# Low-rank branches from unmixed activations, and scan blocks prepared for two heads at once

## The chip, the cores and the metric

One core of one Trainium2 chip runs the whole program. The metric is the device time of one execution in microseconds. Three runs of the kernel before took 2984.91 to 2988.6 us, median 2986.44.

## The reference, cut to what matters

Two blocks run one after the other on 512 tokens of width 1024, in fp32: a first block of neighbourhood attention, gated convolution and MLP, then two layers, each feed-forward, mixer, feed-forward. The mixer of the first of these layers is RWKV-7 time mixing, and only that is touched here:

```
xx = x_prev - x
xr, xw, xk, xv, xa, xg = [x + xx * mu[i] for i in range(6)]
r, k, v = xr @ w_r, xk @ w_k, xv @ w_v              # 1024 x 1024
w = -softplus(-(w0 + tanh(xw @ w1) @ w2)) - 0.5     # rank 64
a = sigmoid(a0 + (xa @ a1) @ a2)                    # rank 64
g = sigmoid(xg @ g1) @ g2                           # rank 128
...
S = S * w_t + (S @ -kk_t) b_t + v_t k_t             # scan over 512 tokens, 16 heads of 64
y = S @ r_t
```

Each of the six inputs is its own mixture of u = x and d = x_prev - x, with a factor mu per channel.

## The kernel before, in words

Activations lie with channels on partitions: eight chunks of 128 channels, and the time mixing works on two halves of 256 tokens each (`hf`). Large products split both operands into a high and a low fp32r part and use three multiplications; the low-rank products are plain fp32, which the profile shows as two records each.

`rwkv` (L1100) is a set of generators. A planner, `_Emit`, keeps a cost model of each engine, decides when a generator has its next turn, and so fixes the order in which instructions are written; the tile framework then places them. At run time each engine works its queue in that order, and SP issues all DMAs in order. `need` and `until` let other generators run while the main line would wait.

The main line walks through `ORDER` (L1107): for each half K, W, A, R, V, G. `mix_task` (L1160) runs ahead of it and makes the mixtures chunk by chunk. For K, R and V `mix_chunk` makes u + mu d on VectorE in an `h` tile, then ScalarE copies the high part and GpSimd or VectorE subtracts the low one. For W, A and G (the `LORA` branches) it makes the mixture alone, on VectorE, straight into half of a tile of the pool `a`. `lora1` (L1203) multiplies eight such chunks by w1, a1 or g1, eight multiplications a branch. The second factors follow in `decay_task`, `a_task` and `g_task`. `token_major` and `receptance` do K, V and R; their weights come in tiles `wr`, which ScalarE copies to `wh` and VectorE or GpSimd subtracts to `wl`.

Results are spilled to DRAM and fetched again by `prep(q, j)` (L1358): half the heads (`q`) and 128 tokens (`j`), eight in all. Of two heads that share 128 partitions, head `e` lies in partitions 64e to 64e + 63. Per block of 64 tokens (`c`) and per head VectorE makes four products of 64 partitions: r and kk by the decay into `E`, b and k2 by the inverse decay into `bk`, where the two heads' parts stand in opposite order. Tiles `E` are one per head, since their other 64 partitions take the masked products of TensorE afterwards. `inverse(j)` then inverts triangular blocks on GpSimd, by way of DRAM; `scan_task` walks over the blocks; `gn_task` normalizes, and `w_o` projects a half once both scans have come far enough. The pool `a` has 56 tiles; `prep_task` waits until 12 are free.

In the profile nearly all operations other than multiplications carry the line of the helper that records them (L290, L292), so shapes and tile names tell them apart.

Of the kernel before, what the change touches and what calls it, by code (L numbers as in the profile page):

```python
# [20 lines left out]
P = 128  # L21
T = 512
D = 1024
DC = D // P
# [10 lines left out]
_VEC = {}  # L35
# [262 lines left out]
def tile_net(ctx: ExitStack, tc: tile.TileContext, a: dict, out: bass.AP, dbg=None, stop=None):  # L298
# [34 lines left out]
    def S():  # L333
        return spool.tile([P, 64], F32, tag="s", name=nm("s"))
# [762 lines left out]
    def rwkv(on_h):  # L1097
# [2 lines left out]
        live[0] = BEFORE  # L1100

        ud = {}
        oka, half_tile = S(), [None]
        vt.tensor_scalar(out=oka[:, 0:8], in0=vec[:, _VEC["k_a"] : _VEC["k_a"] + 8], scalar1=-1.0, scalar2=1.0, op0=MUL, op1=ADD)
        R_, W_, K_, V_, A_, G_ = range(6)
        LORA = {W_: ("w1", 64), A_: ("a1", 64), G_: ("g1", 128)}

        ORDER = [(0, K_), (0, W_), (0, A_), (0, R_), (0, V_), (0, G_), (1, K_), (1, W_), (1, A_), (1, R_), (1, V_), (1, G_)]
        LAST_A = [x for x in ORDER if x[0] == 0][-1]
        mixed = {x: [] for x in ORDER}  # L1110
        made, used, flags = [0], [0], {}
        AHEAD = 8
        EARLY = 10
        MARGIN = [2]
        turn = [0]

# [4 lines left out]
        def mix_chunk(i, c, hf):  # L1121

            uc, dc, m = ud[hf, c][:, 0:256], ud[hf, c][:, 256:512], V("mu", 8 * i + c)
            if i in LORA:
                if c % 2 == 0:
                    half_tile[0] = A()
                t_ = half_tile[0][:, HALF[c % 2]]
                vt.scalar_tensor_tensor(out=t_, in0=dc, scalar=m, in1=uc, op0=MUL, op1=ADD)
                return (t_,)
            t_ = H()  # L1130
            vt.scalar_tensor_tensor(out=t_, in0=dc, scalar=m, in1=uc, op0=MUL, op1=ADD)
            x_ = A(F32R)
            hi, lo = x_[:, 0:256], x_[:, 256:512]
            split_into((hi, lo), t_, HW, eng=vt if c % 3 == 2 else gp)
            return hi, lo
# [22 lines left out]
                free(*h, n=2)  # L1158

        def mix_task():  # L1160
            for hf, i in ORDER:
                for c in range(DC):
                    while made[0] >= used[0] + (AHEAD if (hf, i) in ORDER[:4] else 8) or (hf, c) not in ud or not room(MARGIN[0]):
                        yield 0.25
                    mixed[hf, i].append(mix_chunk(i, c, hf))
                    made[0] += i not in LORA or c % 2
                    if hf == 1 and i == ORDER[-1][1]:
                        free(ud[1, c])
                    if hf == 0 and (hf, i) == LAST_A:
                        free(ud[0, c])  # L1170
                    yield mixed[hf, i][max(c - 2, 0)]

        for hf in range(2):
# [26 lines left out]
            mixed[hf, i] = None  # L1200
            return pss

        def lora1(w, m, hf, i):  # L1203
            ps = PS()
            for k in range(DC):
                x_ = take(hf, i, k)[0]
                w_ = w[k * m // 512][:, k * m % 512 : k * m % 512 + m]
                em.need(ps[:m, HW], w_, x_)
                mm(ps[:m, HW], w_, x_, k == 0, k == DC - 1)
                if k % 2:  # L1210
                    used[0] += 1
                    free(x_)
            mixed[hf, i] = None
            return ps

        def kkrow(wh):
# [58 lines left out]
            free(x_)  # L1275
            flags["lg", hf] = True

        def load_raw(src, n, rows=P):

            ts = [A() for _ in range(0, n, 512)]  # L1280
            for i, t_ in enumerate(ts):
                dma(out=t_[:rows, :], in_=src[:, 512 * i : 512 * i + 512])
            return ts

        def lora2(hf, w, rows, mid, done_):
            ws = load_raw(a[w], 1024, rows)
            for n in range(DC):
                p2 = PS()
                w_ = ws[n // 4][0:rows, (n % 4) * 128 : (n % 4 + 1) * 128]
                yield (p2, w_, mid)  # L1290
                mm(p2[:, HW], w_, mid[0:rows, :])
                done_(n, p2)
            free(*ws)

        def a_task(hf, ps):

            x_ = A()
            mid = x_[:, HW]
            copy(mid[0:64, :], ps[0:64, HW])

            def fin(n, p2):
                t_ = H()
                act.activation(out=t_, in_=p2[:, HW], func=AF.Sigmoid, bias=V("a0", n))
                spill(ad[hf][n], t_)

            yield from lora2(hf, "a2", 64, mid, fin)
            free(x_)
            flags["a", hf] = True

        def g_task(hf, ps):  # L1310

            x_ = A()
            mid = x_[:, HW]
            act.activation(out=mid, in_=ps[:, HW], func=AF.Sigmoid)

            def fin(n, p2):
                t_ = H()
                copy(t_, p2[:, HW])
                spill(gd[hf][n], t_)

            yield from lora2(hf, "g2", 128, mid, fin)
            free(x_)
            flags["g", hf] = True

# [33 lines left out]
        def prep(q, j):  # L1358
# [25 lines left out]
            F[q, j], ARB[q, j] = ff, rb_t  # L1384
            f4 = ff.rearrange("p (c q f) -> p c q f", c=2, q=4)
            rb4 = rb_t.rearrange("p (c q f) -> p c q f", c=2, q=4)
            for c in range(2):
                bk, cg = A(), 2 * j + c
                b4 = bk.rearrange("p (q f) -> p q f", q=4)
                for e in range(2):  # L1390
                    pr = slice(64 * e, 64 * e + 64)
                    ee = A()
                    E[q, e, cg] = ee
                    e4 = ee.rearrange("p (q f) -> p q f", q=4)
                    tt(vt, e4[pr, :, 64:128], tv(r_, pr, c), tv(pp_, pr, c), MUL)
                    tt(vt, e4[pr, :, 1:64], tv(kk, pr, c, 1, 64), tv(pp_, pr, c, 0, 63), MUL)
                    copy(e4[pr, :, 0:1], tv(kk, pr, c, 0, 1))
                    ob, ok = (0, 64) if e == 0 else (64, 0)
                    tt(vt, b4[pr, :, ob : ob + 64], tv(b_, pr, c), tv(ip, pr, c), MUL)
                    tt(vt, b4[pr, :, ok : ok + 64], tv(k2, pr, c), tv(ip, pr, c), MUL)  # L1400
                    yield [k2,]
                yield (bk, *(E[q, e, cg] for e in range(2)))
                pas = [PS(), PS()]
                for p in range(4):
                    for e in range(2):
                        pr = slice(64 * e, 64 * e + 64)
# [12 lines left out]
                copy(BKN[q, cg], pn)  # L1419
                free(bk)  # L1420
            free(kk, b_, ip, pp_)
            f8 = ff.rearrange("p (u f) -> p u f", u=8)
            for e in range(2):
                for b in range(2):
# [93 lines left out]
        def prep_task():  # L1518
            for n in range(8):
                j, q = n // 2, n % 2  # L1520
                hf = j // 2
                while not all(flags.get(n_) for n_ in (("k", hf, q), ("lg", hf), ("a", hf), ("r", hf, q))):
                    yield 0.3
                while n >= prepped[0] + 2 or not room(12):
                    yield 0.3
                em.spawn(prep(q, j))
                yield 0.3
# [191 lines left out]
            free(*(zq[hf, k][i] for k in range(4) for i in range(2)))  # L1719
            em.spawn(post(hf, o, hs, so))  # L1720

        tasks = {W_: decay_task, A_: a_task, G_: g_task}
        raw = {}
        for n, (hf, i) in enumerate(ORDER):
            for nxt in ORDER[n : n + 2]:
                if nxt[1] in LORA and nxt not in raw:
                    w, m = LORA[nxt[1]]
                    raw[nxt] = load_raw(a[w], 8 * m)
            if not hv and n >= EARLY and min(done["z"]) >= 1:
                w_o(0)  # L1730
            if i in LORA:
                em.spawn(tasks[i](hf, lora1(raw[hf, i], LORA[i][1], hf, i)))
                free(*raw[hf, i])
            elif i == K_:
                em.spawn(keys_task(hf, token_major(a["w_k"], K_, hf)))
            elif i == V_:
# [329 lines left out]
def pack(inp):  # L2066
# [46 lines left out]
    w["w_k"] = _wn(rkv[1])  # L2113
    w["w_v"] = _wn(rkv[2])
    w["rwkv_w_o"] = _wt(g["rwkv_w_o_2"][0])
    w["w1"] = _wn(g["rwkv_w1_2"][0], 64)[0]
    w["w2"] = np.ascontiguousarray(np.concatenate([g["rwkv_w2_2"][0], g["rwkv_w0_2"][0][None]], axis=0))
    w["a1"] = _wn(g["rwkv_a1_2"][0], 64)[0]
    w["a2"] = np.ascontiguousarray(g["rwkv_a2_2"][0])
    w["g1"] = _wn(g["rwkv_g1_2"][0], 128)[0]  # L2120
    w["g2"] = np.ascontiguousarray(g["rwkv_g2_2"][0])
# [28 lines left out]
```

## Time and profile before

| | |
|---|---|
| median of three runs | 2986.44 us |
| profiled execution | 2986.91 us |
| its span | 2985.1 us |
| TensorE busy (x: instructions) | 2820.6 us, 94% (x17736) |
| VectorE busy | 1624.0 us, 54% (x2896) |
| ScalarE busy | 1233.9 us, 41% (x2141) |
| GpSimd busy | 692.3 us, 23% (x802) |
| mean granted TensorE clock | 0.968 |

The shares are means over the whole program; the time mixing takes a part of it with shares of its own. In the profile PE is TensorE, DVE is VectorE, ACT is ScalarE, POOL is GpSimd, SP issues the DMAs. A granted clock of 1.0 is 2.4 GHz, 0.5 is 1.2 GHz.

### The profile page before, as it was taken

To read this page: it belongs to the slowest core of one execution; us is meant where nothing else is said; L and a number is where in the kernel's file an instruction comes from. 1 tells how busy PE (TensorE), PEld (TensorE's weight loads), DVE (VectorE), ACT (ScalarE), POOL (GpSimd) and SP (SyncE) were. 2 spreads that over 40 slices of the span, in tenths; PEclk is the share of its full clock that TensorE was granted. 3 is DMA by queue.
4 is the path that set the end of the run, shared out by engine and by line. 5 is a ranking of instruction groups with operands and counts; after the bars stand their busy time and mean duration, and the time that the engine had idled before them with its cause. 6 is when DMAs were issued, how large, how long until landed. Compare 5 with 4: busy or idle time off the path is not lost. (4 is left out here: it accounts for less than half of the span.)

```text
span 2985.1 us, 45687 instructions
## 1 busy us (share of the span) xinstructions
PE 2820.6 (94%) x17736; PEld 2442.6 (82%) x17736; DVE 1624.0 (54%) x2896; ACT 1233.9 (41%) x2141; POOL 692.3 (23%) x802
## 2 busy tenths in 40 slices
PE   9999999999999989878789989998999989999998
PEld 7788888889888877656679989998888877888887
DVE  6545443335334486955676665366234476852336
ACT  4532333333333345544455544344233347733333
POOL 0022211111111143444355110111111134420111
PEclk9999999999999999988889999999999999999999
DMA  5333333332333455645565556343334432323334
GB/s 187 88 94 97 114 99 99 98 95 81 108 99 121 121 184 185 205 142 159 166 177 167 179 168 180 111 145 111 98 98 122 124 114 75 102 80 101 111 109 155
DMA packets 179408, 378.31 MB, mean 127 GB/s; under 512 B 57204, under 2 KB 81908, under 8 KB 179192
## 3 DMA queue, kind: packets, MB, share of 16 engines
q1 hardware_dynamic: 179192, 375.40, 41.6%
q8 instruction: 140, 2.29, 0.3%
q14 instruction: 76, 0.62, 0.1%
HBM read 342.04 MB, written 29.36 MB: 124 GB/s over the span
## 5 line engine op out<-in xcount | busy, mean ns | idle before, releaser
L379 PE MATMUL m<-a,wh 128*128 128x256 f32 (+1 forms) x8512 | 2061.5, 334 | 15.1 <-DVE a L290 7.2
L379 PEld LDWEIGHTS m<-a,wh 128*128 128x128 f32 x8512 | 1461.6, 192 | 178.7 <-issue 13.9
L379 PE MATMUL m<-a,wl 128*128 128x256 f32 (+1 forms) x4256 | 1414.1, 333 | 2.9 <-DVE wl L290 2.9
L290 ACT ACTIVATE wh<-wr 128x1024 fp32r<-128x1024 f32 (+2 forms) x585 | 606.0, 1038 | 1190.7 <-PE m L379 714.8
L290 DVE TENSOR_TENSOR wl<-wr,wh 128x1024 fp32r<-128x1024 f32 (+2 forms) x547 | 679.7, 1244 | 458.9 <-ACT wh L290 456.0
L379 PEld LDWEIGHTS m<-a,wl 128*128 128x128 f32 x4256 | 815.8, 192 | 78.4 <-DVE wl L290 3.5
L290 POOL TENSOR_TENSOR a<-a,a 128x256 f32<-128x256 f32 (+5 forms) x312 | 359.6, 1159 | 1633.5 <-ACT a L290 1317.4
L290 DVE TENSOR_TENSOR a<-m,a 128x512 f32<-128x512 f32 (+1 forms) x324 | 198.5, 614 | 629.6 <-PE m L379 618.9
L290 ACT ACTIVATE a<-a 128x512 f32<-128x512 f32 (+6 forms) x515 | 239.6, 481 | 121.3 <-DVE a L290 88.9
L379 PE MATMUL m<-wh,a 128*128 128x512 f32 x800 | 268.0, 409 | 12.5 <-DVE a L290 10.3
L379 PEld LDWEIGHTS m<-wh,a 128*128 128x128 f32 x800 | 155.7, 195 | 49.3 <-DVE a L290 12.5
L290 DVE TENSOR_TENSOR a<-a,a 128x256 f32<-128x256 f32 (+3 forms) x305 | 164.2, 567 | 36.0 <-ACT a L290 28.9
L379 PE MATMUL m<-wl,a 128*128 128x512 f32 x400 | 162.5, 406 | 0.0
L290 DVE SCALAR_TENSOR_TENSOR a<-a,vec,a 128x256 fp32r<-128x256 f32 (+4 forms) x246 | 144.9, 629 | 9.2 <-ACT a L290 8.4
L290 POOL TENSOR_TENSOR a<-h,a 128x256 fp32r<-128x256 f32 x80 | 68.3, 856 | 342.6 <-ACT a L290 328.0
L290 POOL TENSOR_TENSOR wl<-wr,wh 128x1024 fp32r<-128x1024 f32 x38 | 95.0, 2502 | 110.3 <-ACT wh L290 103.2
L379 PE MATMUL t<-a,a 64*128 64x128 f32 (+4 forms) x528 | 90.0, 356 | 32.0 <-DVE a L290 16.5
L379 PEld LDWEIGHTS t<-a,a 64*128 64x128 f32 (+3 forms) x528 | 57.4, 198 | 56.5 <-issue 25.6
L290 ACT ACTIVATE a<-t 128x512 f32<-128x512 f32 (+3 forms) x122 | 59.3, 491 | 90.0 <-PE t L379 70.6
L379 PEld LDWEIGHTS m<-wl,a 128*128 128x128 f32 x400 | 78.1, 195 | 16.1 <-issue 0.7
L290 ACT ACTIVATE a<-a,vec 128x256 fp32r<-128x256 f32 (+2 forms) x108 | 60.3, 565 | 47.2 <-DVE a L290 43.1
L292 ACT ACTIVATE a<-t 128x256 f32<-128x256 f32 (+3 forms) x100 | 45.4, 472 | 80.3 <-PE t L379 60.6
(108 smaller groups left out, 1533.5 us busy)
## 6 DMA issues: line engine op xcount, KB each, us to landing
wr<-in_ffn_w_in_dram SPq DMA_DIRECT2D x204, 512.0 KB, 3.7
wr<-in_ffn_w_out_dram SPq DMA_DIRECT2D x80, 448.0 KB, 3.3
wr<-in_ffn_w_out_dram SPq DMA_DIRECT2D x48, 512.0 KB, 3.6
wr<-in_w_out_t_dram SPq DMA_DIRECT2D x34, 512.0 KB, 3.7
wr<-in_w_mlp_in_dram SPq DMA_DIRECT2D x32, 512.0 KB, 3.6
wr<-in_w_mlp_out_dram SPq DMA_DIRECT2D x32, 512.0 KB, 3.7
wr<-in_w_gate_dram SPq DMA_DIRECT2D x16, 512.0 KB, 3.6
wr<-in_w_k_dram SPq DMA_DIRECT2D x16, 512.0 KB, 4.6
```

The source lines that it names most:

```text
L290: return fn(*args, **kw)
L292: return fn(*args, **kw)
L379: nc.tensor.matmul(out_, lhsT=lhsT, rhs=rhs, start=start, stop=stop)
```

## The change

w1 and a1 become one matrix of 128 columns, and the three low-rank branches no longer get mixtures. With x = u + mu d, x @ w1 = u @ w1 + d @ (mu w1): GpSimd multiplies the raw weights by mu once a half (`lora_w`), and TensorE multiplies u and d each by its matrix into one PSUM tile. W and A share the step `WA_`; the a branch then lies in partitions 64 to 127, and `a_task` and `lora2` work there. The u and d tiles of a half are freed after G's products instead of its mixtures.

In `prep` b and k2 are multiplied by the inverse decay once for all blocks and heads; the products for `E` are made for both heads in one instruction, into the first head's tile; ScalarE copies the upper half to the second head's tile and places the four parts of `bk`. `prep_task` waits for 13 free tiles.

```diff
-        ORDER = [(0, K_), (0, W_), (0, A_), (0, R_), (0, V_), (0, G_), (1, K_), (1, W_), (1, A_), (1, R_), (1, V_), (1, G_)]
+        WA_ = 6
+        ORDER = [(hf, i) for hf in range(2) for i in (K_, WA_, R_, V_, G_)]
+        MIXED = [x for x in ORDER if x[1] in (K_, R_, V_)]
...
-        EARLY = 10
+        EARLY = 8
...
-            if i in LORA:
-                if c % 2 == 0:
-                    half_tile[0] = A()
-                t_ = half_tile[0][:, HALF[c % 2]]
-                vt.scalar_tensor_tensor(out=t_, in0=dc, scalar=m, in1=uc, op0=MUL, op1=ADD)
-                return (t_,)
...
+        def lora_w(name, idx):
+            ws = load_raw(a[name], 1024)
+            ms = []
+            for i, w_ in enumerate(ws):
+                m_ = A()
+                w4, m4 = (t_.rearrange("p (k i m) -> p k i m", k=4, i=len(idx)) for t_ in (w_, m_))
+                for x, id_ in enumerate(idx):
+                    c = _VEC["mu"] + 8 * id_ + 4 * i
+                    mu = vec[:, c : c + 4].unsqueeze(2).broadcast_to([P, 4, 128 // len(idx)])
+                    tt(gp, m4[:, :, x, :], w4[:, :, x, :], mu, MUL)
+                ms.append(m_)
+            return ws, ms
+
+        def lora1(hf, ws, ms):
             ps = PS()
             for k in range(DC):
-                x_ = take(hf, i, k)[0]
-                w_ = w[k * m // 512][:, k * m % 512 : k * m % 512 + m]
-                em.need(ps[:m, HW], w_, x_)
-                mm(ps[:m, HW], w_, x_, k == 0, k == DC - 1)
...
+                em.until(lambda: (hf, k) in ud)
+                for i, t_ in enumerate((ws, ms)):
+                    w_, x_ = t_[k // 4][:, (k % 4) * 128 : (k % 4 + 1) * 128], ud[hf, k][:, HALF[i]]
+                    em.need(ps[:, HW], w_, x_)
+                    mm(ps[:, HW], w_, x_, k == 0 and i == 0, k == DC - 1 and i == 1)
+            free(*ws, *ms)
             return ps
...
+            ki = A()
+            tt(vt, b_, b_, ip, MUL)
+            tt(vt, ki, k2, ip, MUL)
+            free(ip)
+            yield [ki,]
+            both = slice(0, 128)
             for c in range(2):
-                bk, cg = A(), 2 * j + c
+                bk, e0, e1, cg = A(), A(), A(), 2 * j + c
+                tt(vt, e4[:, :, 64:128], tv(r_, both, c), tv(pp_, both, c), MUL)
+                tt(vt, e4[:, :, 1:64], tv(kk, both, c, 1, 64), tv(pp_, both, c, 0, 63), MUL)
+                copy(e4[:, :, 0:1], tv(kk, both, c, 0, 1))
                 for e in range(2):
                     pr = slice(64 * e, 64 * e + 64)
-                    tt(vt, e4[pr, :, 64:128], tv(r_, pr, c), tv(pp_, pr, c), MUL)
-                    tt(vt, e4[pr, :, 1:64], tv(kk, pr, c, 1, 64), tv(pp_, pr, c, 0, 63), MUL)
-                    copy(e4[pr, :, 0:1], tv(kk, pr, c, 0, 1))
                     ob, ok = (0, 64) if e == 0 else (64, 0)
-                    tt(vt, b4[pr, :, ob : ob + 64], tv(b_, pr, c), tv(ip, pr, c), MUL)
-                    tt(vt, b4[pr, :, ok : ok + 64], tv(k2, pr, c), tv(ip, pr, c), MUL)
-                    yield [k2,]
+                    copy(b4[pr, :, ob : ob + 64], tv(b_, pr, c))
+                    copy(b4[pr, :, ok : ok + 64], tv(ki, pr, c))
+                copy(e1[64:128, :], e0[64:128, :])
...
-                while n >= prepped[0] + 2 or not room(12):
+                while n >= prepped[0] + 2 or not room(13):
...
         for n, (hf, i) in enumerate(ORDER):
+            if i == K_:
+                lw[WA_] = lora_w("wa1", (W_, A_))
+            elif i == V_:
+                lw[G_] = lora_w("g1", (G_,))
...
+            if i == WA_:
+                ps = lora1(hf, *lw[WA_])
+                em.spawn(decay_task(hf, ps))
+                em.spawn(a_task(hf, ps))
+            elif i == G_:
+                em.spawn(g_task(hf, lora1(hf, *lw[G_])))
+                free(*(ud[hf, c] for c in range(DC)))
```

## Rows read from the trace of the kernel before

**Rows 1.** Windows: stretch, length, busy us (x) by engine, PEclk, DMA share, GB/s
```profile
1060.00:1180.00 120.00, 98.93 (x548) 81.08 (x547) 92.83 (x173) 56.81 (x104) 50.64 (x48) 0.90 0.55 178
1180.00:1290.00 110.00, 84.92 (x445) 67.49 (x443) 93.60 (x166) 52.40 (x112) 56.30 (x84) 0.91 0.59 184
1290.00:1480.00 190.00, 154.80 (x1561) 120.49 (x1562) 115.15 (x244) 91.68 (x191) 78.76 (x121) 0.81 0.56 165
1480.00:1600.00 120.00, 106.12 (x1109) 95.10 (x1108) 92.97 (x201) 68.69 (x150) 71.42 (x120) 0.89 0.61 176
1060.00:1600.00 540.00, 444.77 (x3657) 364.16 (x3656) 394.55 (x784) 269.59 (x555) 257.12 (x371) 0.87 0.58 174
```

**Rows 2.** Waits of PE, 1060 to 1600: total us, times, longest us
```profile
PE t L379 <- DVE a L290: 23.2, 13, 4.8
PE t L379 <- ACT a L290: 14.6, 2, 13.7
PE m L379 <- DVE a L290: 14.1, 6, 7.0
PE m L379 <- ACT a L290: 11.9, 3, 9.6
PE t L379 <- POOL a L290: 5.5, 1, 5.5
PE t L393 <- DVE a L290: 4.2, 2, 2.1
PE t L393 <- POOL a L292: 4.2, 2, 2.4
PE t L379 <- DVE h L290: 4.0, 3, 1.9
```

**Rows 3.** Groups by shape, DVE, 1060 to 1740: busy us, mean ns, idle before
```profile
L290 DVE TENSOR_TENSOR a<-a,a 64x256 f32<-64x256 f32 x96 | 43.6, 478 | 0.7 <-DMA bon<-a 0.2
L290 DVE SCALAR_TENSOR_TENSOR a<-a,vec 128x256 f32<-128x256 f32 x48 | 27.1, 595 | 0.1
L290 DVE TENSOR_TENSOR a<-a,a 64x252 f32<-64x252 f32 x32 | 21.4, 670 | 0.0
L290 DVE TENSOR_TENSOR a<-a,a 128x512 f32<-128x512 f32 x8 | 7.6, 954 | 15.7 <-ACT a L290 15.7
```

**Rows 4.** Groups by shape, ACT, 1060 to 1740
```profile
L290 ACT ACTIVATE a<-a 128x256 f32<-128x256 f32 x46 | 18.4, 409 | 9.0 <-DVE a L290 8.7
L290 ACT ACTIVATE a<-a 128x512 f32<-128x512 f32 x24 | 14.7, 624 | 9.4 <-DMA a<-lg 6.5 <-DVE a L290 2.9
L290 ACT ACTIVATE a<-a 64x4 f32<-64x4 f32 x32 | 6.5, 202 | 2.2 <-DMA bon<-a 1.8
```

**Rows 5.** Groups by shape, POOL, 1060 to 1740
```profile
L290 POOL TENSOR_TENSOR a<-a,a 128x256 f32<-128x256 f32 x28 | 26.2, 938 | 28.0 <-ACT a L290 27.2
L292 POOL TENSOR_TENSOR a<-a,s 128x512 f32<-128x512 f32 x16 | 20.0, 1250 | 38.5 <-DVE s L292 30.9 <-ACT a L292 6.0 <-ACT wh L290 1.5
```

**Rows 6.** Timeline of PE, low-rank products, half 0: start us, us, idle before
```profile
1131.45 7.12 PE L379 MATMUL m<-a,a 128*64 128x256 f32 x32 [2.18 <-DVE a L290]
...
1235.61 5.46 PE L379 MATMUL m<-a,a 128*128 128x256 f32 x16 [2.00 <-ACT a L290]
```

**Rows 7.** Timeline of DVE and POOL around 1200 us
```profile
1197.65 5.00 DVE L290 TENSOR_TENSOR a<-a,a 64x256 f32<-64x256 f32 x8
...
1199.09 2.60 POOL L290 TENSOR_TENSOR wl<-wr,wh 128x1024 fp32r<-128x1024 f32 x1 [4.51 <-DMA wr<-in_w_v_dram]
...
1221.48 2.87 DVE L290 TENSOR_TENSOR a<-a,a 64x256 f32<-64x256 f32 x8
```

**Rows 8.** Timeline of ACT and PE around 1290 us
```profile
1291.79 1.06 ACT L290 ACTIVATE wh<-wr 128x1024 fp32r<-128x1024 f32 x1 [12.06 <-DMA wr<-in_w_r_dram]
...
1293.61 2.66 PE L379 MATMUL t<-a,a 64*128 64x128 f32 x14 [13.71 <-ACT a L290]
```

**Rows 9.** DMA issues: out<-in, KB each, median us to landing
```profile
a<-in_w_dram SPq DMA_DIRECT2D x2, 256.0 KB, 5.2
```

More of the change, by code (lines that the diff above doesn't have):

```diff
@@ L1102, in rwkv @@
         ud = {}
-        oka, half_tile = S(), [None]
+        oka = S()
         vt.tensor_scalar(out=oka[:, 0:8], in0=vec[:, _VEC["k_a"] : _VEC["k_a"] + 8], scalar1=-1.0, scalar2=1.0, op0=MUL, op1=ADD)
         R_, W_, K_, V_, A_, G_ = range(6)
-        LORA = {W_: ("w1", 64), A_: ("a1", 64), G_: ("g1", 128)}
-        ORDER = [(0, K_), (0, W_), (0, A_), (0, R_), (0, V_), (0, G_), (1, K_), (1, W_), (1, A_), (1, R_), (1, V_), (1, G_)]
-        LAST_A = [x for x in ORDER if x[0] == 0][-1]
-        mixed = {x: [] for x in ORDER}
+        WA_ = 6
+        ORDER = [(hf, i) for hf in range(2) for i in (K_, WA_, R_, V_, G_)]
+        MIXED = [x for x in ORDER if x[1] in (K_, R_, V_)]
+        mixed = {x: [] for x in MIXED}
         made, used, flags = [0], [0], {}
         AHEAD = 8
-        EARLY = 10
+        EARLY = 8
         MARGIN = [2]
@@ L1160, in mix_task @@
         def mix_task():
-            for hf, i in ORDER:
+            for hf, i in MIXED:
                 for c in range(DC):
-                    while made[0] >= used[0] + (AHEAD if (hf, i) in ORDER[:4] else 8) or (hf, c) not in ud or not room(MARGIN[0]):
+                    while made[0] >= used[0] + (AHEAD if (hf, i) in MIXED[:2] else 8) or (hf, c) not in ud or not room(MARGIN[0]):
                         yield 0.25
                     mixed[hf, i].append(mix_chunk(i, c, hf))
[L1166 to L1170, printed above, removed]
+                    made[0] += 1
                     yield mixed[hf, i][max(c - 2, 0)]
@@ L1201, in token_major @@
             return pss
-        def lora1(w, m, hf, i):
+        def lora_w(name, idx):
[11 more added lines that the diff above has]
+        def lora1(hf, ws, ms):
             ps = PS()
             for k in range(DC):
-                x_ = take(hf, i, k)[0]
-                w_ = w[k * m // 512][:, k * m % 512 : k * m % 512 + m]
-                em.need(ps[:m, HW], w_, x_)
-                mm(ps[:m, HW], w_, x_, k == 0, k == DC - 1)
[L1210 to L1213, printed above, removed]
+                em.until(lambda: (hf, k) in ud)
[4 more added lines that the diff above has]
+            free(*ws, *ms)
             return ps
@@ L1276, in decay_task, with load_raw @@
             flags["lg", hf] = True
-        def load_raw(src, n, rows=P):
+        def load_raw(src, n, rows=slice(0, P)):
             ts = [A() for _ in range(0, n, 512)]
             for i, t_ in enumerate(ts):
-                dma(out=t_[:rows, :], in_=src[:, 512 * i : 512 * i + 512])
+                dma(out=t_[rows, :], in_=src[:, 512 * i : 512 * i + 512])
             return ts
@@ L1288, in lora2 @@
                 p2 = PS()
-                w_ = ws[n // 4][0:rows, (n % 4) * 128 : (n % 4 + 1) * 128]
+                w_ = ws[n // 4][rows, (n % 4) * 128 : (n % 4 + 1) * 128]
                 yield (p2, w_, mid)
-                mm(p2[:, HW], w_, mid[0:rows, :])
+                mm(p2[:, HW], w_, mid[rows, :])
                 done_(n, p2)
@@ L1298, in a_task @@
             mid = x_[:, HW]
-            copy(mid[0:64, :], ps[0:64, HW])
+            copy(mid[64:128, :], ps[64:128, HW])
             def fin(n, p2):
@@ L1304, in fin @@
                 spill(ad[hf][n], t_)
-            yield from lora2(hf, "a2", 64, mid, fin)
+            yield from lora2(hf, "a2", slice(64, 128), mid, fin)
             free(x_)
@@ L1319, in fin @@
                 spill(gd[hf][n], t_)
-            yield from lora2(hf, "g2", 128, mid, fin)
+            yield from lora2(hf, "g2", slice(0, 128), mid, fin)
             free(x_)
@@ L1386, in prep @@
             rb4 = rb_t.rearrange("p (c q f) -> p c q f", c=2, q=4)
-            for c in range(2):
-                bk, cg = A(), 2 * j + c
-                b4 = bk.rearrange("p (q f) -> p q f", q=4)
+            ki = A()
[4 more added lines that the diff above has]
+            both = slice(0, 128)
+            for c in range(2):
+                bk, e0, e1, cg = A(), A(), A(), 2 * j + c
+                E[q, 0, cg], E[q, 1, cg] = e0, e1
+                b4, e4 = (t_.rearrange("p (q f) -> p q f", q=4) for t_ in (bk, e0))
+                tt(vt, e4[:, :, 64:128], tv(r_, both, c), tv(pp_, both, c), MUL)
+                tt(vt, e4[:, :, 1:64], tv(kk, both, c, 1, 64), tv(pp_, both, c, 0, 63), MUL)
+                copy(e4[:, :, 0:1], tv(kk, both, c, 0, 1))
                 for e in range(2):
                     pr = slice(64 * e, 64 * e + 64)
-                    ee = A()
-                    E[q, e, cg] = ee
-                    e4 = ee.rearrange("p (q f) -> p q f", q=4)
-                    tt(vt, e4[pr, :, 64:128], tv(r_, pr, c), tv(pp_, pr, c), MUL)
-                    tt(vt, e4[pr, :, 1:64], tv(kk, pr, c, 1, 64), tv(pp_, pr, c, 0, 63), MUL)
-                    copy(e4[pr, :, 0:1], tv(kk, pr, c, 0, 1))
                     ob, ok = (0, 64) if e == 0 else (64, 0)
-                    tt(vt, b4[pr, :, ob : ob + 64], tv(b_, pr, c), tv(ip, pr, c), MUL)
-                    tt(vt, b4[pr, :, ok : ok + 64], tv(k2, pr, c), tv(ip, pr, c), MUL)
-                    yield [k2,]
+                    copy(b4[pr, :, ob : ob + 64], tv(b_, pr, c))
+                    copy(b4[pr, :, ok : ok + 64], tv(ki, pr, c))
+                copy(e1[64:128, :], e0[64:128, :])
                 yield (bk, *(E[q, e, cg] for e in range(2)))
@@ L1420, in prep @@
                 free(bk)
-            free(kk, b_, ip, pp_)
+            free(kk, b_, ki, pp_)
             f8 = ff.rearrange("p (u f) -> p u f", u=8)
@@ L1720, in w_o @@
             em.spawn(post(hf, o, hs, so))
-        tasks = {W_: decay_task, A_: a_task, G_: g_task}
-        raw = {}
+        lw = {}
         for n, (hf, i) in enumerate(ORDER):
[L1725 to L1728, printed above, removed]
+            if i == K_:
+                lw[WA_] = lora_w("wa1", (W_, A_))
+            elif i == V_:
+                lw[G_] = lora_w("g1", (G_,))
             if not hv and n >= EARLY and min(done["z"]) >= 1:
                 w_o(0)
-            if i in LORA:
-                em.spawn(tasks[i](hf, lora1(raw[hf, i], LORA[i][1], hf, i)))
-                free(*raw[hf, i])
+            if i == WA_:
[5 more added lines that the diff above has]
+                free(*(ud[hf, c] for c in range(DC)))
             elif i == K_:
@@ L2115, in pack @@
     w["rwkv_w_o"] = _wt(g["rwkv_w_o_2"][0])
-    w["w1"] = _wn(g["rwkv_w1_2"][0], 64)[0]
+    w["wa1"] = _wn(np.concatenate([g["rwkv_w1_2"][0], g["rwkv_a1_2"][0]], axis=1), 128)[0]
     w["w2"] = np.ascontiguousarray(np.concatenate([g["rwkv_w2_2"][0], g["rwkv_w0_2"][0][None]], axis=0))
-    w["a1"] = _wn(g["rwkv_a1_2"][0], 64)[0]
     w["a2"] = np.ascontiguousarray(g["rwkv_a2_2"][0])
```

## The prediction

> **What bounds the kernel now.** I read the busy time by stretches first, then who ended TensorE's waits in the same stretch, then the rows of the operations that the change touches, by shape. Over the whole span TensorE is the bound. The part that the change touches, 1060 to 1600 us (the time mixing's projections and the first scans), is another matter: TensorE is busy 444.77 of 540 us there, so 95.2 us are idle, at a granted clock of 0.87 [rows 1]. The reader is to see in the four stages that VectorE is busy 92.83 of 120, 93.60 of 110, 115.15 of 190 and 92.97 of 120 us, ScalarE about half of each. In the second stage VectorE is the fullest engine of all.
>
> Who ended TensorE's idle time [rows 2]: VectorE 23.2 + 14.1 + 4.2 + 4.0 = 45.5 us, which is 48% of the 95.2. ScalarE ended 14.6 + 11.9 = 26.5 us, but in one case each of 13.7 and 9.6 us it was only the last of a chain. Ahead of the 13.7 us ScalarE itself had waited 12.06 us for a weight tile of w_r [rows 8]: the load stood in SP's queue, so its cause is a transfer issued late. That leaves some 3 of 26.5 for plain ScalarE work, and with the 9.6 us about 13%; I work with 11%. GpSimd ended 5.5 + 4.2 = 9.7 us (10%); as it often stands behind ScalarE and VectorE in a chain I take 20%.
>
> The lost clock is a second price of the same waits. Busy time times what is missing of full clock, by stage: 98.93 x 0.10 + 84.92 x 0.09 + 154.80 x 0.19 + 106.12 x 0.11 = 58.6 us [rows 1], or 0.62 us for each idle microsecond. If half of that goes with the idle time that goes, an idle microsecond saved is worth 1.31.
>
> **The change part by part.**
>
> *Mixtures of the low ranks (removed).* 48 VectorE instructions, mean 595 ns: 27.1 us [rows 3]. Half 0's and half 1's share of w and a is 16 each, of g 8 each.
>
> *Block preparation on VectorE.* Eight preparations, all before 1600 us, now issue 96 products of 64x256 at 478 ns and 32 of 64x252 at 670 ns: 43.6 + 21.4 = 65.0 us [rows 3]. After: per preparation two whole products (b and k2 by the inverse decay), 16 x 954 ns = 15.3 us by the row of 128x512, and per block one product for both heads in place of two. Twice the partitions are no more elements per partition, so I price them by the 64-partition rows: 16 x 478 ns = 7.6 us and 16 x 670 ns = 10.7 us. Sum 33.6, so 31.4 us less. VectorE loses 27.1 + 31.4 = 58.5 us of its 394.55. What this is worth to TensorE lies between nothing (each VectorE-ended wait is taken over by the next late thing) and all 45.5 us. I take the 48% share: 58.5 x 0.48 = 28.1 us. Late next where these waits go are the weight splits, whose loads SP issues late [rows 8], and GpSimd's block inverses.
>
> *Placing on ScalarE (added).* Per block four copies of 64x256 and one of 64x512, and one small copy instead of two: 64 x 409 ns = 26.2, 16 x 624 ns = 10.0, minus 16 x 202 ns = 3.2, together 33.0 us [rows 4]. It is also a new wait: the products go from VectorE through ScalarE before TensorE may begin. Behind the copies in ScalarE's queue stand the high parts of the weight splits (VectorE's low parts and then TensorE wait for them) and the PSUM evacuations. The ends are 0 (ScalarE is busy only 269.59 of 540 us [rows 1]) and all 33.0; with the 11% share I charge 3.6 us.
>
> *Scaled weights on GpSimd (added).* Per half four multiplications of 128x256 elements for w and a, two of 128x512 for g: 8 x 938 ns + 4 x 1250 ns = 12.5 us [rows 5]. Ends 0 and 12.5, charged at 20%: 2.5 us. GpSimd also waits for the raw weights to land. The same bytes are loaded in the same number of DMAs as before, but a1's now comes with w1's; a load takes 5.2 us to land [rows 9], and behind the waiting multiplication on GpSimd stand its share of K's weight splits and mixture splits, for which TensorE waits. Four loads make 0 to 21 us of standing, at 20% up to 4.2 us; I take 0, since each pair of matrices is asked for a whole projection ahead.
>
> The row that speaks most against this part is VectorE beside GpSimd. Eight products of 64x256 took 5.00 us while GpSimd ran a split of 2.60 us at 1199.09, and 2.87 us at 1221.48 [rows 7], 0.62 against 0.36 us each. The Trainium skill ("GPSIMD Engine Reference", section "Specifications") says that GpSimd shares its SBUF interfaces with VectorE, and that VectorE instructions with two SBUF inputs contend with it. The trace agrees, and by that rule the 12.5 us would also be taken from VectorE; that is a rival below.
>
> *TensorE.* w and a together keep their 16 multiplications per half, now of 128 columns instead of 64 (32 records in 7.12 us [rows 6]); g goes from 8 to 16 per half, 32 records more in all. At 7.12/32 us a record that is 7.1 us, at g's own 5.46/16 (part of it at the low clock) 10.9. I take 9.0. No mixture has to be ready for them any more; what that saves is in VectorE's share already.
>
> *The rest at nothing.* The a branch in the upper 64 partitions changes no count; the order of projections stays as it was with w and a in one step, and the output projection may start at the same step. The u and difference tiles of a half are held until g's multiplications instead of its last mixture: at most g's 5.46 us [rows 6] later, which a preparation that waits for 13 free tiles would see. It is covered as long as the scan has a finished block ahead. Uncovered it is 5.5 us, once a half.
>
> **Sum.** Idle time: -28.1 + 3.6 + 2.5 = -22.0 us. Clock: 0.31 x 22.0 = -6.8. TensorE's work: +9.0. Together -19.8 us. The profiled execution took 2986.91 us (2985.1 span and 1.8 around it), 0.5 over the median of the three runs, 2986.44. So 2967.1 on the one and 2966.6 on the other; I say 2967. With VectorE's share between 0.35 and 0.7 this case reaches from 2977 (-20.5 + 6.1 idle, x 1.31, + 9) to 2950 (-41.0 + 6.1).
>
> **Rivals.**
>
> A, the waits go altogether: all 45.5 us, and the 13.7 us stall too, because an earlier inverse no longer holds SP's queue. (-59.2 + 6.1) x 1.31 + 7.1 = -62.5, 2924 us. For it: VectorE is fullest just ahead of that stall. Against: the planner lays the order anew, and such a stall can as well appear elsewhere.
>
> B, hidden: only a fifth of the VectorE time reaches TensorE, since ScalarE's, GpSimd's and SP's waits lie just behind. (-11.7 + 6.1) x 1.31 + 9 = +1.7, 2989 us. For it: the third stage is the one with the most idle time (35.2 us), and VectorE is busy only 61% of it [rows 1]; only stages one and two are clearly its own.
>
> C, slower: ScalarE takes over as the engine that is late in the preparation. With a share x of the 33.0 us reaching TensorE the sum is 1.31 x (-28.1 + 2.5 + 33.0x) + 9 = -24.5 + 43.2x. It decides from x = 0.57: beyond that the kernel is slower, at 0.8 it takes 2997, at 1 it takes 3006. For it: every block's two parts now pass ScalarE's one queue, next to weight splits of about 1 us each [rows 8]. Against: ScalarE is busy 52.40 of 110 us in the second stage, 48%, and 33.0 us over the whole 540 add 6%.
>
> D, GpSimd's multiplications block VectorE for their whole length: VectorE saves 46 instead of 58.5 us, 12.5 x 0.48 x 1.31 = 7.9 us less gain, 2975 us. The contended row bears it out in part: the products there lost 2.1 us beside a split of 2.6 us [rows 7]. It is what the rule of the Trainium skill named above would come to at its worst.
>
> **How the numbers follow.** Forecast 0.42, A (below 2950) 0.14, B (2981 to 2993) 0.17, C (above 2993) 0.17, D 0.10. A measurement of this kernel can tell about 0.2% from no change, 6 us. Faster by more than that holds the forecast, A and D: 0.66; within it B: 0.17; slower C: 0.17. The range leaves out the far ends of A and C, about 0.1 each: 2935 to 2998. The forecast's own is 2950 to 2977.
>
> **What would show it.** The mixture rows of 128x256 into a full tile gone (48), the 64x256 and 64x252 products gone, VectorE's busy time about 58 us lower and ScalarE's 33, GpSimd's 12 higher. In the stretch of the projections, TensorE's waits ended by VectorE down from 45.5 to about 20 us, the clock there up. After it the profile should be as before, shifted. Wrong would be: VectorE lower by that much and TensorE's idle time unchanged (B), waits now ended by ScalarE in the preparation's multiplications (C), or a longer stall behind SP's queue.

## The result, and the profile after

The changed kernel takes 3006.89 us (median, 3001.99 to 3010.78), the kernel before 2987.09 in the same comparison: ratio 1.0066, 95% interval 1.0048 to 1.0084. Forecast was 2967, range 2935 to 2998. It is slower, by nearly what it was to gain.

The profiled execution's span went from 2985.1 to 3002.7 us, by 17.6: TensorE's busy time grew by 7.8 (2820.6 to 2828.4), its idle time by 9.8. VectorE is busy 43.1 us less over the whole span, ScalarE 28.0 and GpSimd 4.4 more.

Busy time by stretches, after; columns as in [rows 1]:
```profile
1060.00:1180.00 120.00, 92.45 (x509) 76.75 (x508) 89.01 (x157) 54.05 (x100) 52.75 (x51) 0.84 0.52 172
1180.00:1290.00 110.00, 96.99 (x513) 80.75 (x512) 75.12 (x109) 73.25 (x150) 74.63 (x94) 0.92 0.67 211
1290.00:1480.00 190.00, 150.61 (x1403) 121.82 (x1401) 97.32 (x191) 104.86 (x229) 69.82 (x114) 0.83 0.56 169
1480.00:1600.00 120.00, 88.89 (x1122) 79.47 (x1121) 79.93 (x183) 55.89 (x130) 70.33 (x134) 0.82 0.46 124
```
Only the second stage, where VectorE had been the fullest engine, has more of TensorE at work (84.92 to 96.99 us). The first lost 6.5 us, the third 4.2, the fourth 17.2.

Who ended TensorE's waits there, after, for [rows 2]:
```profile
PE m L379 <- POOL a L290: 13.5, 4, 9.9
PE t L379 <- DVE a L290: 12.2, 5, 5.7
PE t L379 <- ACT a L290: 11.4, 8, 7.6
PE t L379 <- DVE s L292: 10.5, 2, 9.0
PE m L379 <- ACT a L290: 10.1, 5, 3.0
PE t L379 <- DVE h L292: 9.2, 2, 6.1
PE t L393 <- POOL a L292: 8.5, 1, 8.5
PE t L379 <- DMA a<-in_g_dram: 7.3, 2, 5.6
PE m L379 <- DVE a L290: 6.1, 3, 3.0
```
VectorE's two largest rows fell from 37.3 to 18.3 us, but not its sum. [rows 2] shows only the first eight rows of the view; over all rows VectorE ended 50.6 us before and 43.4 after, ScalarE 33.9 and 30.2, GpSimd 9.9 and 27.9, DMAs 0.4 and 9.1. Single long waits have come, ended by a different engine each time, which points to something late upstream of all of them.

The operations themselves, after, by shape, VectorE first; for [rows 3], [rows 4] and [rows 5]. The mixtures that stayed stand in the first row; before, they had
```profile
L290 DVE SCALAR_TENSOR_TENSOR h<-a,vec 128x256 f32<-128x256 f32 x48 | 27.8, 608 | 1.7 <-POOL a L290 1.2
```
and after:
```profile
L290 DVE SCALAR_TENSOR_TENSOR h<-a,vec 128x256 f32<-128x256 f32 x48 | 39.2, 850 | 17.9 <-POOL a L290 13.6 <-ACT a L290 3.9
L290 DVE TENSOR_TENSOR a<-a,a 128x256 f32<-128x256 f32 x55 | 31.9, 589 | 1.9 <-ACT a L290 1.9
L290 DVE TENSOR_TENSOR a<-a,a 128x512 f32<-128x512 f32 x24 | 19.0, 806 | 16.1 <-ACT a L290 16.0
L290 DVE TENSOR_TENSOR a<-a,a 128x252 f32<-128x252 f32 x16 | 8.4, 528 | 0.0
...
L290 ACT ACTIVATE a<-a 64x256 f32<-64x256 f32 x64 | 23.0, 404 | 0.4
L290 ACT ACTIVATE a<-a 64x512 f32<-64x512 f32 x16 | 9.9, 618 | 13.7 <-DVE a L290 13.6
...
L290 POOL TENSOR_TENSOR a<-a,vec 128x512 f32<-128x512 f32 x4 | 6.2, 1565 | 0.7 <-DMA a<-in_g_dram 0.7
L290 POOL TENSOR_TENSOR a<-a,vec 128x256 f32<-128x256 f32 x8 | 5.4, 707 | 2.1 <-DMA a<-in_wa_dram 2.1
```
The counts are those of the forecast and the prices near it: ScalarE's placing 32.9 us (forecast 36.2 before the small copies), GpSimd's scaling 11.6 (12.5).

The view that shows the cause is SP's queue, at the issues that begin a preparation (`a<-kkt`, the key fetch) and a block inverse (`iat<-fsc`). Before, the fourth fetch and the second inverse (start us, us to issue):
```profile
1264.44 0.38 SPq L290 DMA_DIRECT2D a<-kkt  x1
...
1306.24 2.94 SPq L290 DMA_DIRECT2D iat<-fsc  x2
```
After, the third and fourth fetch, then the second inverse:
```profile
1252.16 0.38 SPq L290 DMA_DIRECT2D a<-kkt  x1
...
1329.49 0.63 SPq L290 DMA_DIRECT2D a<-kkt  x1
...
1363.20 1.10 SPq L290 DMA_DIRECT2D iat<-fsc  x2
```
The third fetch is 38 us late (before it was at 1213.96), the fourth 65, the inverse 57. The projections meanwhile run ahead: g's last low-rank product begins at 1417.36 instead of 1474.71. TensorE then waits, first in a projection, later in preparations, the scan and what follows it (timeline of TensorE, idle before in brackets):
```profile
1388.80 1.22 PE L379 MATMUL m<-wh,a 128*128 128x512 f32 x2 [9.90 <-POOL a L290]
...
1447.09 3.33 PE L379 MATMUL t<-a,a 64*128 64x128 f32 x16 [7.61 <-ACT a L290]
...
1506.16 1.11 PE L393 MATMUL t<-cst,a 128*128 128x128 f32 x4 [8.52 <-POOL a L292]
...
1573.08 0.99 PE L379 MATMUL t<-cst,a 128*128 128x1 f32 x4 [9.00 <-DVE s L292]
```
The first of these waits shows one way in which the lateness is paid. The product is one of V's, and it waits for a mixture split (`a<-h,a`) on GpSimd. ScalarE had done its part of that mixture at 1378.11, but the split stood in GpSimd's queue behind operations of the second block inverse (`h<-a,iat`), which now falls into this projection (timeline of GpSimd):
```profile
1387.67 0.40 POOL L290 TENSOR_TENSOR h<-a,iat 128x120 f32<-128x120 f32 x1
1388.03 0.72 POOL L290 TENSOR_TENSOR a<-h,a 128x256 fp32r<-128x256 f32 x1
```
Before, all of TensorE's waits of this kind (`PE m <- POOL a`) came to 0.2 us from 1060 to 1600.

### The profile page after: what moved, and what is told of

Same layout as the page of the kernel before. It is cut to its first block, busy times and chain, and to the rows that moved or that the text cites. A ratio compares the mean times of both kernels' runs of the same rounds, so it can differ in the third digit from the quotient of the medians.

```text
span 3002.7 us, 45719 instructions
## 1 busy us (share of the span) xinstructions
PE 2828.4 (94%) x17768; PEld 2458.4 (82%) x17768; DVE 1580.9 (53%) x2768; ACT 1261.9 (42%) x2205; POOL 696.7 (23%) x814
## 4 chain that ended last, share of the span: by engine, by line
PE 77%; DVE 9%; POOL 4%; issue 4%; ACT 3%; DMA 2%; SPq 1%; DVEq 0%; ACTq 0%; POOLq 0%
PE m L379 70%; PE t L379 5%; DVE a L290 4%; POOL a L290 2%; PE t L393 2%; DVE wl L290 1%; ACT a L290 1%; POOL h L290 1%; DVE s L292 1%; ACT wh L290 1%; DVE h L290 1%; DVE h L292 1%; SPq L290 1%; POOL a L292 0%; DMA wr<-in_w_qkv_dram 0%
## 5 line engine op out<-in xcount | busy, mean ns | idle before, releaser
L290 ACT ACTIVATE a<-a 128x256 f32<-128x256 f32 (+7 forms) x579 | 268.3, 484 | 126.6 <-DVE a L290 102.2
L290 DVE TENSOR_TENSOR a<-a,a 128x256 f32<-128x256 f32 (+2 forms) x225 | 131.1, 597 | 35.3 <-ACT a L290 29.3
L379 PE MATMUL t<-a,a 64*128 64x128 f32 (+4 forms) x528 | 91.6, 361 | 32.1 <-DVE a L290 11.6
L290 ACT ACTIVATE a<-t 128x512 f32<-128x512 f32 (+3 forms) x122 | 59.0, 493 | 59.9 <-PE t L379 43.1
```

The source lines that it names most:

```text
L290: return fn(*args, **kw)
L379: nc.tensor.matmul(out_, lhsT=lhsT, rhs=rhs, start=start, stop=stop)
```

## The experiments

The leading theory, T: the preparations of the second pair of chunks wait for free tiles. A preparation begins when 13 of the pool's 56 tiles are free (12 before); u and difference tiles held until g's multiplications, and four tiles of low-rank weights, leave fewer; mixtures made ahead take what comes free. The count is the planner's, kept while it writes the program: a preparation that misses its tiles is written later, and so stands later in SP's and every engine's queue. Rivals: S, ScalarE's placing is late in the preparation (rival C); L, the low-rank part costs as such. All ratios are to the kernel before on the same chip.

**One part alone.** `lora_only`: the diff without its lines in `prep`, `room(12)` kept.

> The kernel before with the low ranks without mixtures alone; the block preparation and its 12 free tiles are as before. Theory T (tiles): u and difference tiles held until g's multiplications and four tiles of weights each leave the preparations of the second pair of chunks without free tiles, and they start 30 us or more late; the time is then like that of the changed kernel, 1.003 to 1.009 of before, and the third preparation pair's key fetches stand later than 1213.96 and 1264.44 us. Theory S (ScalarE's placing is what is late): this kernel has no placing, so it is faster, 0.992 to 0.998. Theory L (the low-rank part itself costs, by GpSimd's multiplications and TensorE's 9 us): slower, 1.003 to 1.009, but with the preparations on time.

Measured 1.0106 [1.0093, 1.0119], a little more than T gave it; fourth fetch at 1333.05. S is out as the whole cause: there is no placing here.

`prep_only`: the diff's lines in `prep` and `room(13)`, nothing else.

> The kernel before with the block preparation of the changed kernel alone (13 free tiles asked for); mixtures of the low ranks as before. T: one tile more is asked for and more are held at once, so the fourth preparation may still lose the race for tiles: 0.997 to 1.006, the sign by whether its fetch is later than 1264 us. S: as slow as the changed kernel, 1.005 to 1.010, with TensorE's waits ended by ScalarE in the preparation's multiplications. L: faster by what VectorE saves, 0.992 to 0.997.

Measured 1.0108 [1.0095, 1.0122], more than T gave it. This part holds no tile longer for the low ranks than the kernel before, and yet its fourth preparation is as late.

`prep_only_room12`, against `prep_only`:
```diff
-                while n >= prepped[0] + 2 or not room(13):
+                while n >= prepped[0] + 2 or not room(12):
```


> The same, with the preparation asking for 12 free tiles as before: one number differs from prep_only. The engines' work is identical in both. T: the fourth preparation starts on time again, 0.991 to 0.998, and faster than prep_only by 0.3% or more. S and L: no difference from prep_only beyond 0.2%.

Measured 0.9948 [0.9934, 0.9963]. One number, the same operations in another order (only ScalarE's table loads differ: 13 here, 11 in the slow one), and 48 us between them. The fourth fetch and the second inverse in SP's queue, with 13 tiles:
```profile
1331.03 0.44 SPq L290 DMA_DIRECT2D a<-kkt  x1
...
1367.48 1.11 SPq L290 DMA_DIRECT2D iat<-fsc  x2
```
and with 12:
```profile
1263.70 0.45 SPq L290 DMA_DIRECT2D a<-kkt  x1
...
1298.12 2.87 SPq L290 DMA_DIRECT2D iat<-fsc  x2
```

`before_room16`: the kernel before with `room(12)` made `room(16)`.

> The kernel before with one number changed: a preparation waits for 16 free tiles instead of 12. No engine gets more or less to do. T: the preparations of the second pair start later, as in the changed kernel, and the time rises by what lateness alone costs, 1.003 to 1.012. S and L: the start of a preparation is covered by the finished blocks ahead of the scan, 0.999 to 1.002.

Measured 1.0085 [1.0072, 1.0098]: the old kernel, made to start late, loses 25 us. Its fourth fetch and second inverse:
```profile
1336.39 0.43 SPq L290 DMA_DIRECT2D a<-kkt  x1
...
1371.15 1.10 SPq L290 DMA_DIRECT2D iat<-fsc  x2
```
In both late kernels a product of V waits for a split behind the second inverse on GpSimd, as in the changed kernel: 7.98 us in `prep_only`, 16.80 in `before_room16`.

**Both parts, with the preparations on time.** `after_room10`: the changed kernel with `room(13)` made `room(10)`.

> The changed kernel with one number changed: a preparation starts at 10 free tiles instead of 13. T: the fourth preparation's key fetch is back near 1264 us (1329.49 in the changed kernel), the stalls of 1380 to 1580 us go, and what the engines save shows: 0.988 to 0.996 of before. S: as the changed kernel, 1.004 to 1.009. L (the low-rank part costs as such): between the block preparation alone on time, 0.9948, and 1.002.

Measured 1.0032 [1.0020, 1.0044], fourth fetch at 1260.82. On time, and still slower: a miss for T as the only cause, and in no theory's range. Against the changed kernel TensorE's idle time fell by 12.8 us and its busy time rose by 5.5.

`lora_room10`: `lora_only` with 10 for 12.

> The low ranks without mixtures alone, with 10 free tiles asked for instead of 12 (the preparation is the one of before). T: preparations on time, and the part is worth its VectorE time, 27.1 us by the share of 48%, against TensorE's 9.0 and GpSimd's 2.5: 0.994 to 1.000. L: still slower than before by 0.3% or more, with the fourth fetch on time. S: 0.992 to 0.998, the same as the run with 12 (which took 1.0106, so S is out where these differ).

Measured 1.0006 [0.9998, 1.0015], fetch at 1263.86: 30 us better than `lora_only`, but no gain on the kernel before: above T's range and below L's.

`prep_room11`: `prep_only` with 11 for 13.

> The block preparation alone, asking for 11 free tiles (12 took 0.9948, 13 took 1.0108). T: once the fourth preparation is on time nothing more is to be had from an earlier one: 0.992 to 0.997, within 0.3% of the run with 12. A rival, that time follows the start of the preparations all along and not in a step, expects 0.985 to 0.990.

Measured 0.9957 [0.9943, 0.9971], fetch at 1235.08. 29 us earlier than with 12 and no faster: a step, not a slope.

`after_prep_first`: the changed kernel, 13 kept; in `mix_task`:
```diff
-... or (hf, c) not in ud or not room(MARGIN[0]):
+... or (hf, c) not in ud or not room(MARGIN[0] if hf == 0 or prepped[0] >= 4 else 13):
```


> The changed kernel with the other cure: 13 tiles asked for as in it, but mixtures of the second half are made only while 13 tiles are free, until four preparations are done. T: the fourth preparation is on time, the second half's projections wait for their mixtures some us instead: 0.990 to 1.000. If the lateness of the preparations is not the cause: 1.004 to 1.010.

Measured 0.9978 [0.9967, 0.9988], fetch at 1272.37. Cured in another way, the kernel is faster than before; but the preparation's part alone gave 0.9948. Why this cure is worth 26 us and asking for 10 tiles only 10 stays open.

**What the low-rank part costs.** In the changed kernel, `after_room10`, `lora_room10` and `after_prep_first` TensorE stands still ahead of the product of w and a: busy 4.4 to 4.7 of the 20 us from 1120 to 1140, where the kernel before has 17.5.

`no_scaling`, against `after_prep_first`:
```diff
-                    tt(gp, m4[:, :, x, :], w4[:, :, x, :], mu, MUL)
...
-                ms.append(m_)
+                ms.append(w_)
```


> The changed kernel with preparations first (as after_prep_first, 0.9978), and GpSimd's multiplications of the low-rank weights left out: the difference tiles meet the unscaled weights, so w, a and g are other numbers; tiles, loads and TensorE's work stay. Theory G (what the low-rank part costs is GpSimd's 12.5 us, in the way of the mixture splits and the second half's statistics at 1104 to 1144 us): the stall there goes, TensorE's busy time in 1120 to 1140 is back above 12 us from 4.4, and the time falls by 8 to 20 us, 0.991 to 0.995. Theory P (it is TensorE's longer products and the lost filler of mixtures): within 0.2% of after_prep_first, with the stall still there.

Measured 0.9916 [0.9903, 0.9930]: 18 us on `after_prep_first`. TensorE is busy 10.05 us in 1120 to 1140, where 12 had been expected: a little under half of the stall went. What the rest is stays open.

`scaling_on_scalar`: that line as `copy(m4[:, k, x, :], w4[:, k, x, :], V("mu", 8 * id_ + 4 * i + k))` for each of four k.

> The same kernel as after_prep_first, but ScalarE scales the low-rank weights (24 small copies a half, 16 of 64 and 8 of 128 columns) in place of GpSimd's six multiplications. G: part of the gain of no_scaling, 0.993 to 0.998, unless ScalarE's queue now holds the weight splits of the first projection. P: 0.996 to 1.000, the same as after_prep_first.

Measured 0.9969 [0.9956, 0.9981], stall still there (TensorE busy 4.57 us of the 20). It decided nothing: both theories allowed it.

`prep_only_first`: `prep_only_room12` with the same restraint on mixtures, 12 for 13.

> The block preparation alone with 12 free tiles (0.9948) and the second half's mixtures waiting while fewer than 12 tiles are free. The preparations are on time in both, so T expects no more than 0.3% between them: 0.992 to 0.998. If mixtures held back starve the projections it is above 0.998.

Measured 0.9975 [0.9965, 0.9986]: within what was said, but 8 us worse than without it. The restraint has a price of its own where it isn't needed (the two intervals just miss each other).

`g_mixed_first`: `after_prep_first` with g's mixtures, raw weights and 8 multiplications a half put back.

> The changed kernel with preparations first, and g alone back on its mixtures: its two halves take 8 multiplications each instead of 16, its weights aren't scaled, the u and difference tiles go with its last mixture. T: the fourth preparation is on time by a wider margin; TensorE 9 us less, VectorE 8 more, so 0.993 to 0.998. If w and a are what costs (the stall at 1120 to 1140 us), it stays there and the time is within 0.2% of after_prep_first.

Measured 0.9984 [0.9975, 0.9992], TensorE busy 3.85 us of the 20. The stall belongs to w and a. TensorE's busy time fell by 7.1 us (2822.9 to 2815.8), but its idle time rose by 11.3.

`late_scaling`, against `after_prep_first`; g's weights likewise, and with the eight unscaled products of `lora1` first:
```diff
-                lw[WA_] = lora_w("wa1", (W_, A_))
+                lw[WA_] = load_raw(a["wa1"], 1024)
...
-                ps = lora1(hf, *lw[WA_])
+                ps = lora1(hf, *lora_w(lw[WA_], (W_, A_)))
```


> The changed kernel with preparations first (0.9978); the raw weights are loaded where they were, but GpSimd scales them only when the projection ahead of the low ranks has been issued, and TensorE takes the eight products with unscaled weights first. The same instructions, in another order. Theory Q (the scaling stood in GpSimd's queue, waiting for its late weights, with mixture splits and statistics behind it): 8 us or more faster, 0.990 to 0.9955, near no_scaling's 0.9916. Theory E (the 12.5 us of work itself, in contention with VectorE): as after_prep_first, 0.996 to 1.000.

Measured 0.9925 [0.9912, 0.9938], 2965.79 us: faster than both kernels. The same work in another order gives 16 us. The number is Q's, not all of Q's reason. GpSimd's timeline of `after_prep_first`:
```profile
1101.68 2.39 POOL L290 TENSOR_TENSOR wl<-wr,wh 128x1024 fp32r<-128x1024 f32 x1 [7.29 <-DMA xsc<-a]
1104.03 3.07 POOL L290 TENSOR_TENSOR a<-a,vec 128x256 f32<-128x256 f32 x4
1107.06 2.40 POOL L290 TENSOR_TENSOR a<-h,a 128x256 fp32r<-128x256 f32 x2
```
and of `late_scaling`:
```profile
1101.93 2.43 POOL L290 TENSOR_TENSOR wl<-wr,wh 128x1024 fp32r<-128x1024 f32 x1 [7.27 <-DMA xsc<-a]
1104.33 0.92 POOL L290 TENSOR_TENSOR a<-h,a 128x256 fp32r<-128x256 f32 x1
```
The scaling did not wait; it began as the split ended. It stood in front: the mixture splits behind it (`a<-h,a`) came 2.7 us later, and the second half's statistics came later too. TensorE's product of w and a began at 1142.18 there (timeline, idle before in brackets):
```profile
1125.30 1.01 PE L379 MATMUL t<-cst,a 128*128 128x1 f32 x4 [6.73 <-POOL a L290]
1133.43 1.22 PE L379 MATMUL t<-h,cst 128*128 128x256 f32 x2 [6.06 <-DVE h L292]
1138.04 1.12 PE L393 MATMUL t<-cst,a 128*128 128x128 f32 x4 [3.38 <-ACT a L290]
1142.18 9.69 PE L379 MATMUL m<-a,a 128*128 128x256 f32 x32 [3.02 <-DVE a L290]
```
and in `late_scaling` at 1137.57:
```profile
1120.32 1.01 PE L379 MATMUL t<-cst,a 128*128 128x1 f32 x4 [6.18 <-POOL a L290]
1128.50 0.70 PE L379 MATMUL t<-h,cst 128*128 128x256 f32 x2 [0.67 <-DVE h L292]
1134.05 1.12 PE L393 MATMUL t<-cst,a 128*128 128x128 f32 x4 [4.85 <-ACT a L290]
1137.57 8.71 PE L379 MATMUL m<-a,a 128*128 128x256 f32 x32 [2.41 <-DVE a L290]
```
4.6 us earlier. The rest of the gain lies in the later order, which fell out anew; no row here accounts for it singly. The fourth fetch is also 21.6 us earlier (1250.80), though in `prep_room11` an earlier one was worth nothing. Of the 10.9 us between the two profiled executions only 3.5 are TensorE's idle time; 7.4 are its busy time for the same 17768 multiplications, at a mean granted clock of 0.967 and 0.973.

`late_alone`: the same edit on the changed kernel, without the restraint.

> The changed kernel as it stands, 13 tiles asked for and no priority, with the scaling late as in late_scaling. If tiles are a cause of their own, the fourth preparation is still late (fetch near 1320 to 1330 us) and the kernel still slower than before or equal, 0.999 to 1.006; Q gives it 3 to 12 us on the changed kernel, 1.0066. If the late scaling was the whole cause: 0.990 to 0.996.

Measured 1.0095 [1.0079, 1.0110], fourth fetch at 1333.88. Slower than was expected, and the clearest sign that the tiles are a cause of their own: where the fourth preparation is late, a better start of the projections (TensorE is busy 11.14 of the 20 us here) gains nothing; this kernel is slower than the changed one by 9 us.

`late_scaling_12`: `late_scaling` with 12 for 13 in both places.

> late_scaling with 12 tiles in place of 13 in both the preparation's question and the mixtures' restraint. T and Q: the fourth preparation a little earlier, the same within 0.2% of late_scaling, 0.989 to 0.996; it tests how much of such a time is the order that falls out.

Measured 0.9938 [0.9926, 0.9951], as expected: 4 us from `late_scaling`, which the two intervals don't separate.

All kernels by their fourth key fetch:

| fourth fetch, us | kernels | ratio |
|---|---|---|
| 1329 to 1336 | changed, `lora_only`, `prep_only`, `before_room16`, `late_alone` | 1.0066 to 1.0108 |
| 1235 to 1276 | before (1264.44) and the eleven others | 0.9916 to 1.0032 |

No kernel lies between, in either column. Within a row the fetch does not order the times.

## Why the prediction was wrong

**The step that failed** is "The rest at nothing": tiles held longer cost "at most g's 5.46 us [rows 6] later", "covered as long as the scan has a finished block ahead". A preparation that misses its tiles does not wait for the one release that it missed. In the planner's count it waits until 13 are free at once, and mixtures made ahead, which ask for 2, take the tiles that come free meanwhile (holding these back cured it: `after_prep_first`). So it was 65 us late, not 5.5. Nor was it covered: the second inverse came 57 us late, and lateness alone costs 25 us (`before_room16`) to 48 (`prep_only` against `prep_only_room12`; why nearly twice as much stays open). I had priced a missed tile as a duration, when it was a threshold.

**The prepared blocks were right.** By the prediction's shares the part is 1.31 x (-31.4 x 0.48 + 3.6) = -15.0 us; on time it measured -15.5 (0.9948). In the profile of `prep_only_room12` the terms fit as well: TensorE's idle time fell by 12.4 us (forecast 11.5), its busy time by 2.1 (clock, forecast 3.6). Only the share was larger than 0.48, for VectorE's busy time fell by 22.6 us and not 31.4. Rival C was wrong: the same placing is in the fast kernel.

**The low ranks were wrong in size.** By the same shares: 1.31 x (-27.1 x 0.48 + 2.5) + 9.0 = -4.8; on time it measured +1.8 (`lora_room10`). The term that failed there is the clock, which was to follow the idle time. TensorE's idle time fell by 15.5 us (164.5 to 149.0), more than the 10.5 forecast. But its busy time rose by 19.4 (2820.6 to 2840.0; mean granted clock 0.968 and 0.963), where +9.0 of work and -3.3 of clock had been forecast. The low-rank products themselves take only 2.4 us more (from 1060 to 1740, 28.3 and 30.7). A part of this goes by "Scaled weights on GpSimd", charged 2.5 us and nothing for what stands behind them, as far as the other kernels show it: taken out of `after_prep_first` they gave 18 us, put later 16 (in the profiles 12.1 and 10.9, of which 8.4 and 7.4 are TensorE's busy time). The rest stays open. They stood where TensorE had little other work, ahead of a chain through GpSimd, VectorE, ScalarE and TensorE.

**Rival D shows in single operations, not in the sum.** VectorE was to lose 58.5 us and lost 43.1. What it gave back lies most of all in the first row of its groups: the 48 mixtures that stayed took 850 ns each, before 608 (27.8 us for the same 48), 11.4 us more. But this is not the scaling's doing. In `after_prep_first`, and in `no_scaling`, which leaves the multiplications out, the same row is
```profile
L290 DVE SCALAR_TENSOR_TENSOR h<-a,vec 128x256 f32<-128x256 f32 x48 | 36.9, 803 | 9.1 <-POOL h L290 2.9 <-issue 2.0 <-ACT a L290 1.4
```
```profile
L290 DVE SCALAR_TENSOR_TENSOR h<-a,vec 128x256 f32<-128x256 f32 x48 | 35.8, 777 | 7.9 <-POOL a L290 7.4
```
and VectorE's whole busy time is 1571.8 and 1571.2 us: 0.6 for D's 12.5. `prep_only`, which scales nothing either, has 769 ns, and `lora_room10`, which scales, 639. What these mixtures lost came with the new order; which operations they then stood beside is not shown. In `after_prep_first`, while GpSimd scales from 1104.03 to 1107.10, VectorE's timeline has:
```profile
1104.28 0.84 DVE L290 SCALAR_TENSOR_TENSOR h<-a,vec 128x256 f32<-128x256 f32 x1
1105.04 0.83 DVE L290 TENSOR_TENSOR h<-cst,s 128x256 f32<-128x256 f32 x1
1105.79 0.83 DVE L290 SCALAR_TENSOR_TENSOR a<-a,vec,a 128x256 f32<-128x256 f32 x1
```
and in `late_scaling`, where these two fall for the most part into a gap between two of GpSimd's splits (1105.25 to 1106.05):
```profile
1105.45 0.41 DVE L290 TENSOR_TENSOR h<-cst,s 128x256 f32<-128x256 f32 x1
1105.78 0.47 DVE L290 SCALAR_TENSOR_TENSOR a<-a,vec,a 128x256 f32<-128x256 f32 x1
```
The same two operations take about twice as long beside the scaling. So does a mixture beside a split: the one at 1104.57 in `late_scaling` took 0.96 us. The Trainium skill ("GPSIMD Engine Reference", section "Specifications") names contention for VectorE instructions with two SBUF inputs; the 0.83 against 0.41 us agrees. `late_scaling` has the same multiplications (10.6 us of GpSimd) and is the fast one.

**With both causes mended** the sum comes out, by luck: -19.8 us forecast, and the span of `late_scaling` is 2965.4 against 2985.1, -19.7. TensorE's idle time fell by 14.6 us and not 22.0; its busy time fell by 5.1, where clock and work together were to add 2.2. Two misses of some 7 us cancel, and the restraint on mixtures, which the forecast kernel did not have, is in it too.

## What to carry to other kernels

Where a stage starts on a count of free buffers, a change that holds one more of them, or asks for one more, is a threshold and not a duration: look for who takes the buffers that come free one at a time, and price the miss as the wait for that taker to stop. Test it by that one number, which changes only the order of the operations. And work moved to an idle engine belongs behind what that engine feeds to the bound, not in front of it; here that place was worth 16 us.

## What the runs showed that I had not expected

Asking for 13 free tiles in place of 12, in two kernels of the same operations, moved the whole span by 47.6 us (3018.2 to 2970.6): 39.2 of it TensorE's idle time (191.3 to 152.1), 8.4 its busy time (2826.9 to 2818.5) at a mean granted clock of 0.959 and 0.970. That would be 0.21 us of busy time for each idle microsecond; the prediction took 0.31. But no such rate holds from pair to pair, though in each the multiplications are the same (profiled executions, us):

| from | to | TensorE idle | TensorE busy |
|---|---|---|---|
| `prep_only` | `prep_only_room12` | -39.2 | -8.4 |
| before | `before_room16` | +25.6 | +1.0 |
| changed | `after_room10` | -12.8 | +5.5 |
| `after_prep_first` | `late_scaling` | -3.5 | -7.4 |
| `after_prep_first` | `no_scaling` | -3.7 | -8.4 |

A late preparation is paid for mostly in idle time, the misplaced scaling mostly in busy time. A price per idle microsecond, which the prediction used, has no support here; what sets the share is not shown.
